# Weight tiles split two ahead, norm operands in two operations, and the first squares added on VectorE

## The chip, the cores and the metric

The kernel runs on one core of a Trainium2 chip. The metric is the device time of one launch in microseconds; it was 2138.77 us before (median of 3 runs, 2133.90 to 2140.38). The engines are named as in the profile: PE is TensorE (matrix multiplication), DVE is VectorE, ACT is ScalarE, POOL is GpSimd, SP issues the transfers between HBM and on-chip memory (SBUF). Each engine works through its own list of instructions in order and waits at an instruction until its inputs are there.

## What is computed

One inference step of a two-layer decoder, with width 1024, on a prompt of 512 rows and on 8 samples of 4 rows that have 256 earlier rows each in a paged cache. All of it is fp32. Cut to its structure:

```python
def trunk(x, pe, past):
    h = x
    for i in range(2):
        h = h + 0.5 * swiglu(rmsnorm(h, ffn1_norm[i]), w1, w3, w2)      # 1024 -> 2816 -> 1024
        xn = rmsnorm(h, mix_norm[i])
        if i == 0: mix = gmlp_mix(xn, w_in, v_norm, w_s, b_s, w_out)    # (u * spatial(v)) @ w_out
        else:      mix = forgetting_attention(rmsnorm(xn @ w_q), *kv, past) @ w_o
        h = h + mix
        h = h + 0.5 * swiglu(rmsnorm(h, ffn2_norm[i]), w1, w3, w2)
        h = h + sigmoid(rmsnorm(h, ple_norm[i]) @ w_gate) * (pe[i] @ w_proj)
        if i == 0: kv = shared_kv(h, kv_norm, w_kvf, b_f, k_norm)       # K, V, log-forget, once
    return h, kv

def rmsnorm(x, g): return x * rsqrt(mean(x * x) + 1e-6) * g
```

The outputs are h for the prompt and for the samples, K, V and the log-forget values of both, and the v rows of the gMLP for the samples.

## The kernel before, in words

Activations are kept feature-major: `h` is 8 chunks of 128 features by 544 columns (512 prompt rows and 32 sample rows, so both go through the weights together). A weight tile is 128 x 1024, eight blocks of 128 x 128, one for each chunk of the input.

An fp32 product is made of three passes with operands in two parts. The high part is the value rounded to the matrix engine's fp32r format, the low part is the remainder, and `mm` adds high x high (L233), high weight x low input (L237) and low weight x high input (L239), each in two column pieces (256 and 288): 48 matmuls for one tile of output. So each weight tile is *split* in the kernel, by a cast on ACT (L190) and a subtraction on DVE (L191), and so is each input (`split_pair`, L277 on ACT and L278 on DVE).

Weight tiles come in one stream for the whole program (`prepare`, `take`). `self.ahead` holds three distances, in tiles, counted from the tile that PE is about to use: how far ahead tiles are split, how far ahead the sums of tiles are made, and how far ahead raw tiles are loaded. Raw tiles, split tiles, inputs and chunks of `h` share one pool of 44 buffers of 128 x 1088 ("big" in the profile); a split 128 x 1024 tile takes two. A load on SP waits until its buffer is free, and everything behind it on SP waits with it.

The stages are: FFN 1 of layer A (0 to about 360 us), gMLP (to 590; its output tiles at 515 to 565), FFN 2, the gated embedding and the shared K/V (985 to 1126; tiles of V at 1061 to 1124), FFN 1 of layer B (to 1450), queries and attention (1490 to 1625), its output projection (1625 to 1702), FFN 2 and the embedding. The insides of the FFNs (Strassen-like, seven products for eight, with sums of weight tiles on DVE at L176) run in an order written by hand, with distances (2, 3, 6) of their own. Outside them a scheduler with a model of the engines sets the order.

A norm is applied in two halves. The gain goes into the input ahead of the product: `prep` makes the operand of a chunk as soon as the chunk of `h` is ready: it scales on ACT (L290) into a temporary, and splits that (L277, L278). The factor 1/sqrt(mean) goes onto the product afterwards. It comes from squares on ACT (L316), added up chunk by chunk on POOL (L318, `ssq`), the sum over partitions by PE (L354), and a chain ACT L332, DVE L335, L338, L339. At the start all 8 chunks of `h` are there at once, and the program does 8 preps and 8 squares together.

```python
box = {"x": {c: self.prep(h[c], G_FFN1 + c) for c in range(NC_)}, "f": [], "acc": self.st()}
self._split()
for c in range(NC_):
    self.ssq(box["acc"], h[c], first=c == 0)
```

Other lines that are spoken of: L418 and L484 (first steps behind the products of an FFN), L646 (gMLP output added to `h`), L750 and L769 (V and K taken out of PE's accumulators), L808 to L812 and L862 to L880 (log-forget sums), L941 (queries normed), L1144 to L1146 (the projection's three passes), L1156 and L1165 (its result added to `h`).

Of the kernel before, what the change touches and what calls it, by code (L numbers as in the profile page):

```python
# [22 lines left out]
F32 = mybir.dt.float32  # L23
F32R = mybir.dt.float32r
I32 = mybir.dt.int32
AF = mybir.ActivationFunctionType
ALU = mybir.AluOpType
# [54 lines left out]
def whole(p):  # L82

    return p[:].rearrange("p a b -> p (a b)")[:, 512 - CUT:512 - CUT + T]


class Builder:
# [37 lines left out]
    def set_stream(self):  # L125
        self.chain, self.pending, self.bg, self.pages = None, [], [], {}
        self.aps, self.raws = [], {}
        self.pieces, self.sums, self.split = [], {}, {}
        self.p_next = self.p_split = self.p_sum = self.a_load = 0
        self.ahead = (1, 1, 3)  # L130
        self.pins = 0

    def flat(self, n, dt=F32):
# [151 lines left out]
    def prep(self, h, gcol, pair=None, cols=slice(0, T)):  # L285

        pair = self.big(F32R) if pair is None else pair
        g = self.gain(gcol)
        x = self.tmp()[:, cols]
        self.nc.scalar.activation(x, h[:, cols], AF.Copy, scale=g)  # L290
        self.split_pair(pair, x, cols)
        return pair

    def forms(self, h, gcol, n, xs):
# [103 lines left out]
    def ffn(self, h, box, gcol, rstd, on_chunk):  # L398

        nc, eng = self.nc, mybir.EngineType  # L400
        self.ahead = (2, 3, 6)
        first, xs, xf = [], self.pairs(box), box["f"]

        def more(n):
            if len(xf) < min(n, NKP):
                xf.append(self.forms(h, gcol, len(xf), xs))
        for f in range(2):
            if rstd is None:
                p1, rstd = self.tile_rstd(xs, box["acc"])
            else:  # L410
                p1 = self.tile_mm(xs)
            more(2 * f + 1)
            p3 = self.tile_mm(xs)
            more(2 * f + 2)

            def gate(p1=p1, p3=p3):
                a, b = self.tmp(), self.tmp()
                nc.vector.tensor_tensor(a, whole(p1), rstd, ALU.mult)  # L418
                nc.scalar.activation(a, a, AF.Silu)
                nc.vector.tensor_tensor(b, whole(p3), rstd, ALU.mult)  # L420
                nc.vector.tensor_tensor(b, b, a, ALU.mult)
                pair = self.big(F32R)
                self.split_pair(pair, b)
                first.append((pair[:, 0, :], pair[:, 1, :]))
            self.evac(gate)
        assert len(first) == 2
        with self.tc.manual_schedule(engines={eng.PE, eng.Activation, eng.DVE, eng.Pool}):
            self.ffn_steps(h, xf, rstd, first, on_chunk)
        self.ahead = (1, 1, 3)
        self.pins = 2  # L430
        return rstd

# [741 lines left out]
    def build(self):  # L1174
        nc, i, o = self.nc, self.i, self.o
        self.set_stream()

        def plain(aps):
            for ap in aps:
                self.add_plain(ap)  # L1180

        def ple_units(n):
            for c in range(NC_):
                self.add_plain(i["wg"][n, c])
                if c < 2:
                    self.add_plain(i["wp"][n, c])

        self.ffn_pieces(0)
        plain([i["win"][NC_ + c] for c in range(NC_)] + [i["win"][c] for c in range(NC_)])
        plain(i["wout"][c] for c in range(NC_))  # L1190
        self.ffn_pieces(1)
        ple_units(0)
        plain([i["wf"]] + [i["wkv"][c] for c in range(2 * NC_)])
        self.ffn_pieces(2)
        plain(i["wq"][c] for c in range(NC_))
        plain([i["woh"][k, c] for k in range(2) for c in range(NC_ // 2)] + [i["wo"][c] for c in range(NC_)])
        self.ffn_pieces(3)
        ple_units(1)

        self.eps = self.const.tile([P, 1], F32, name="eps")  # L1200
        nc.vector.memset(self.eps, EPS)
        warm = self.sm(1)
        nc.scalar.copy(warm, self.eps)
        self._load()
        self.g = self.const.tile([P, NG], F32, name="gains")
        nc.scalar.dma_start(out=self.g, in_=i["gains"])
        hp = [self.big() for _ in range(NC_ // 2)]
        h = [hp[c // 2][:, c % 2, :] for c in range(NC_)]
        for c in range(NC_):
            nc.sync.dma_start(out=h[c], in_=i["x"][c])  # L1210
            if c == 2:
                self._load()
        self._split()
        self.ones = self.const.tile([P, 32], F32, name="ones")
        nc.gpsimd.memset(self.ones, 1.0)
        self.onesr = self.const.tile([P, P], F32R, name="onesr")
        nc.gpsimd.tensor_copy(self.onesr, self.ones[:, 0:1].broadcast_to([P, P]))
        self.c = self.const.tile([P, NCONST], F32, name="consts")
        self.pt = self.const.tile([1, NB * NPAGE], I32, name="pt")
        self.ident = self.c[:, C_ID:C_ID + P]  # L1220
        self.identr = self.const.tile([P, P], F32R, name="identr")
        self.neg = self.const.tile([P, 384], F32R, name="neg")
        self.ks = self.const.tile([P, NH, NS], F32, name="ks")

        box = {"x": {c: self.prep(h[c], G_FFN1 + c) for c in range(NC_)}, "f": [], "acc": self.st()}
        self._split()
        for c in range(NC_):
            self.ssq(box["acc"], h[c], first=c == 0)

        def constants():  # L1230
            yield
            nc.sync.dma_start(out=self.c, in_=i["consts"])
            nc.sync.dma_start(out=self.pt, in_=i["pt"])
            passed = self.big()[:].rearrange("p a b -> p (a b)")
            nc.sync.dma_start(out=passed[:, :NPASS], in_=i["passed"])
            yield
            nc.gpsimd.tensor_copy(self.identr, self.ident)
            nc.gpsimd.tensor_copy(self.neg, passed[:, C_NEG:C_NEG + 384])
        self.bg.append(constants())

        on, nxt = self.next_norm(h, G_MIX)
        self.ffn(h, box, G_FFN1, None, on)
        box = nxt
        on, nxt = self.next_norm(h, G_FFN2, early=3)
        self.gmlp(h, box, on)
        box = nxt
        on, nxt = self.next_norm(h, G_PLE)
        self.ffn(h, box, G_FFN2, None, on)
        box = nxt
        on, nxt = self.next_norm(h, G_KV)  # L1250
        self.bg.append(self.past())
        self.ple(h, box, 0, on)
        box = nxt
        box, rstd = self.kv(h, box, G_FFN1 + 8)
        on, nxt = self.next_norm(h, G_MIX + 8)
        self.ffn(h, box, G_FFN1 + 8, rstd, on)
        box = nxt
        on, nxt = self.next_norm(h, G_FFN2 + 8)
        self.attention(self.pairs(box), box["acc"], h, on)
        box = nxt  # L1260
        on, nxt = self.next_norm(h, G_PLE + 8)
        self.ffn(h, box, G_FFN2 + 8, None, on)
        box = nxt
        self.ple(h, box, 1, lambda c: nc.sync.dma_start(out=o["y"][c], in_=h[c]))
# [114 lines left out]
```

## Time and profile before

| | before |
|---|---|
| median of 3 runs | 2138.77 us (2133.90 to 2140.38) |
| profiled execution | 2137.89 us, span 2135.8 us, mean granted PE clock 0.988 |
| PE busy | 2078.1 us (97%), 57.7 us idle |
| DVE, ACT, POOL busy | 1523.3, 979.5, 179.2 us |
| chain that ended last | PE 89%, DVE 6%, ACT 3% |
| moved | 237.94 MB, mean 111 GB/s |

A row of waits reads: the instruction that waited, the releasing engine and tile and line; total us, times, the longest. A row of groups reads: line, engine, operation, shapes, how often, then busy us and the mean ns of one, then the idle time ahead of them and who ended it. A row of the timeline or the chain starts with the time and the length.

### The profile page before, as it was taken

To read this page: it belongs to the slowest core of one execution; us is meant where nothing else is said; L and a number is where in the kernel's file an instruction comes from. 1 tells how busy PE (TensorE), PEld (TensorE's weight loads), DVE (VectorE), ACT (ScalarE), POOL (GpSimd) and SP (SyncE) were. 2 spreads that over 40 slices of the span, in tenths; PEclk is the share of its full clock that TensorE was granted. 3 is DMA by queue.
4 is the path that set the end of the run, shared out by engine and by line. 5 is a ranking of instruction groups with operands and counts; after the bars stand their busy time and mean duration, and the time that the engine had idled before them with its cause. 6 is when DMAs were issued, how large, how long until landed. Compare 5 with 4: busy or idle time off the path is not lost.

```text
span 2135.8 us, 38870 instructions
## 1 busy us (share of the span) xinstructions
PE 2078.1 (97%) x16364; PEld 2033.1 (95%) x16364; DVE 1523.3 (71%) x1886; ACT 979.5 (46%) x1456; POOL 179.2 (8%) x233
## 2 busy tenths in 40 slices
PE   6999999999999999999989999999999899999999
PEld 5999999999999999999989999999876899999999
DVE  6877787556687777766688777786365687777864
ACT  6443344523544344465355344445264654443461
POOL 2000000310100000041140000001041300000010
PEclk9999999999999999999999999999999999999999
DMA  4232324312223222422183322326367322323331
GB/s 158 82 117 70 109 91 138 100 43 80 70 99 109 80 103 90 140 90 79 58 313 135 109 99 90 109 87 210 116 190 259 103 77 93 105 83 109 109 110 43
DMA packets 93776, 237.94 MB, mean 111 GB/s; under 512 B 9490, under 2 KB 27442, under 8 KB 93602
## 3 DMA queue, kind: packets, MB, share of 16 engines
q1 hardware_dynamic: 93458, 235.42, 33.2%
q8 instruction: 129, 2.11, 0.4%
q14 instruction: 45, 0.37, 0.1%
q10 hardware_dynamic: 144, 0.04, 0.0%
HBM read 218.94 MB, written 16.49 MB: 110 GB/s over the span
## 4 chain that ended last, share of the span: by engine, by line
PE 89%; DVE 6%; ACT 3%; issue 1%; DMA 1%; POOL 0%; SPq 0%; ACTq 0%; DVEq 0%; POOLq 0%
PE ps L476 33%; PE ps L233 14%; PE ps L239 14%; PE ps L237 14%; PE pb L476 5%; DVE big L278 1%; DVE big L191 1%; ACT big L190 1%; PE ps L1144 1%; PE ps L1146 1%; PE ps L1145 1%; DVE big L176 1%; ACT big L277 1%; PE ps L990 1%; PE ps L992 0%
## 5 line engine op out<-in xcount | busy, mean ns | idle before, releaser
L476 PE MATMUL ps<-big,big 128*128 128x272 f32 x5760 | 749.9, 289 | 10.1 <-ACT tmp L484 5.1
L476 PEld LDWEIGHTS ps<-big,big 128*128 128x128 f32 x5760 | 735.6, 189 | 11.7 <-ACT tmp L484 6.4
L191 DVE TENSOR_TENSOR big<-big,big 128x1024 fp32r<-128x1024 f32 (+2 forms) x541 | 596.7, 1106 | 102.0 <-ACT big L190 101.4
L190 ACT CAST big<-big 128x1024 fp32r<-128x1024 f32 (+2 forms) x541 | 489.4, 932 | 282.4 <-DVE big L176 275.9
L233 PE MATMUL ps<-big,big 128*128 128x256 f32 (+1 forms) x2768 | 580.6, 291 | 22.3 <-ACT big L277 11.5
L239 PE MATMUL ps<-big,big 128*128 128x256 f32 x2768 | 575.2, 290 | 6.4 <-DVE big L191 6.3
L237 PE MATMUL ps<-big,big 128*128 128x256 f32 x2768 | 577.4, 289 | 3.2 <-DVE big L278 3.1
L233 PEld LDWEIGHTS ps<-big,big 128*128 128x128 f32 x2768 | 447.6, 190 | 26.3 <-ACT big L277 12.0
L237 PEld LDWEIGHTS ps<-big,big 128*128 128x128 f32 x2768 | 451.1, 191 | 4.9 <-DVE big L278 4.9
L239 PEld LDWEIGHTS ps<-big,big 128*128 128x128 f32 x2768 | 446.9, 190 | 8.9 <-DVE big L191 8.2
L318 POOL TENSOR_TENSOR st<-st,tmp 128x544 f32<-128x544 f32 (+1 forms) x70 | 92.0, 1314 | 1644.8 <-ACT tmp L316 1644.2
L176 DVE TENSOR_TENSOR big<-big,big 128x1024 f32<-128x1024 f32 x160 | 195.1, 1219 | 0.0
L515 DVE SCALAR_TENSOR_TENSOR big<-ps,big 128x544 f32<-128x544 f32 x160 | 115.6, 723 | 95.5 <-PE ps L239 95.4
L278 DVE TENSOR_TENSOR big<-tmp,big 128x544 fp32r<-128x544 f32 (+1 forms) x132 | 108.7, 829 | 60.2 <-ACT big L277 59.0
L484 ACT COPY tmp<-ps 128x544 f32<-128x544 f32 x120 | 73.7, 614 | 146.0 <-PE ps L476 145.8
L476 PE MATMUL pb<-big,big 128*128 128x272 f32 x960 | 127.1, 288 | 0.0
L448 ACT ACTIVATE big<-big 128x544 f32<-128x544 f32 x80 | 52.8, 660 | 161.8 <-DVE big L445 160.4
L476 PEld LDWEIGHTS pb<-big,big 128*128 128x128 f32 x960 | 123.2, 188 | 0.0
L445 DVE TENSOR_TENSOR big<-big,st 128x1088 f32<-128x1088 f32 x80 | 103.3, 1291 | 9.9 <-ACT big L498 8.4
L290 ACT ACTIVATE tmp<-big,gains 128x544 f32<-128x544 f32 (+1 forms) x80 | 56.0, 703 | 115.7 <-DVE big L515 44.4
L277 ACT CAST big<-tmp 128x544 fp32r<-128x544 f32 (+1 forms) x132 | 80.6, 614 | 54.7 <-DVE tmp L303 21.5
L278 DVE TENSOR_TENSOR big<-big,big 128x544 fp32r<-128x544 f32 (+1 forms) x96 | 70.2, 731 | 29.0 <-ACT big L277 28.7
(185 smaller groups left out, 1257.8 us busy)
## 6 DMA issues: line engine op xcount, KB each, us to landing
big<-in_w SPq DMA_DIRECT2D x160, 512.0 KB
big<-in_w2a SPq DMA_DIRECT2D x64, 512.0 KB
big<-in_w2b SPq DMA_DIRECT2D x32, 384.0 KB
big<-in_w13p SPq DMA_DIRECT2D x16, 512.0 KB
big<-in_win SPq DMA_DIRECT2D x16, 512.0 KB
big<-in_wg SPq DMA_DIRECT2D x16, 512.0 KB
big<-in_wkv SPq DMA_DIRECT2D x16, 512.0 KB
big<-in_ck SPq DMA_DIRECT2D x16, 512.0 KB
```

The lines of the kernel that those rows point to most:

```text
L176: self.nc.vector.tensor_tensor(t, a, b, ALU.add if op == "+" else ALU.subtract)
L190: self.nc.scalar.copy(hi, src)
L191: self.nc.vector.tensor_tensor(lo, src, hi.bitcast(F32), ALU.subtract)
L233: i = nc.tensor.matmul(out[:, a:b], wh, xh[:, a:b], start=s, stop=False)
L237: nc.tensor.matmul(out[:, a:b], wh, xl[:, a:b], start=False, stop=False)
L239: nc.tensor.matmul(out[:, a:b], wl, xh[:, a:b], start=False, stop=e)
L277: self.nc.scalar.copy(pair[:, 0, cols], src)
L278: self.nc.vector.tensor_tensor(pair[:, 1, cols], src, pair[:, 0, cols].bitcast(F32), ALU.subtract)
L318: nc.gpsimd.tensor_tensor(acc[:, cols], acc[:, cols], sq, ALU.add)
L445: tt(g, g, rstd.unsqueeze(1).broadcast_to([P, 2, T]), ALU.mult)
L476: nc.tensor.matmul(dst[w], a[:, c], b, start=k in "152" and kp == 0 and n == 0, stop=kp == NKP - 1 and n == 2, skip_group_check=True)
L515: nc.vector.scalar_tensor_tensor(h[c], whole(out), 0.5, h[c], ALU.mult, ALU.add)
```

## The change

Three edits. Outside the FFNs the distances become (2, 2, 4) for (1, 1, 3): a tile is split two tiles before it is used, and loaded four before. `prep` takes two operations for three: ACT writes the scaled chunk straight into the fp32r high part (L289), and DVE makes the low part as `h * gain - high` in one operation (L290, with the gain as a column); the temporary is gone. And the 7 additions of the first squares go from POOL (L318) to DVE (L1231); their squares are now on L1229.

```diff
@@ set_stream, and the same again at the end of ffn @@
-        self.ahead = (1, 1, 3)
+        self.ahead = (2, 2, 4)
@@ prep @@
         pair = self.big(F32R) if pair is None else pair
         g = self.gain(gcol)
-        x = self.tmp()[:, cols]
-        self.nc.scalar.activation(x, h[:, cols], AF.Copy, scale=g)
-        self.split_pair(pair, x, cols)
+        self.nc.scalar.activation(pair[:, 0, cols], h[:, cols], AF.Copy, scale=g)
+        self.nc.vector.scalar_tensor_tensor(
+            pair[:, 1, cols], h[:, cols], g, pair[:, 0, cols].bitcast(F32), ALU.mult, ALU.subtract)
         return pair
@@ at the start @@
         for c in range(NC_):
-            self.ssq(box["acc"], h[c], first=c == 0)
+            sq = box["acc"] if c == 0 else self.tmp()
+            nc.scalar.activation(sq, h[c], AF.Square)
+            if c:
+                nc.vector.tensor_tensor(box["acc"], box["acc"], sq, ALU.add)
```

ACT has 1329 rows in place of 1409, DVE 1881 for 1873, POOL 199 for 206, SP 663 as before. Three places show how the order moves. The numbers in the names of buffers differ between the two programs; what counts is which buffer is used where.

The first is ACT at the start of the program (big_86 to big_89 hold the chunks of `h`, two each). Before:

```order
4 L290 ACTIVATE tmp_114<-big_86,gains 128x544
5 L316 ACTIVATE st_153<-big_86 128x544
6 L190 CAST big_100<-big_82 128x1024
7 L290 ACTIVATE tmp_119<-big_86,gains 128x544
8 L290 ACTIVATE tmp_124<-big_87,gains 128x544
9 L277 CAST big_113<-tmp_114 128x544
10 L277 CAST big_118<-tmp_119 128x544
...
24 L316 ACTIVATE tmp_168<-big_88 128x544
25 L277 CAST big_148<-tmp_149 128x544
...
29 L316 ACTIVATE tmp_177<-big_89 128x544
30 L190 CAST big_182<-big_180 128x1024
```

And after the change:

```order
4 L1229 ACTIVATE st_137<-big_86 128x544
5 L190 CAST big_100<-big_82 128x1024
6 L1229 ACTIVATE tmp_143<-big_86 128x544
7 L1229 ACTIVATE tmp_146<-big_87 128x544
8 L289 ACTIVATE big_113<-big_86,gains 128x544
9 L289 ACTIVATE big_116<-big_86,gains 128x544
...
19 L289 ACTIVATE big_134<-big_89,gains 128x544
20 L190 CAST big_138<-big_93 128x1024
21 L1229 ACTIVATE tmp_161<-big_89 128x544
22 L190 CAST big_166<-big_164 128x1024
```

The last square moves from row 29 to row 21, the last high part from row 25 to row 19, and three squares now stand ahead of the first operand where one did.

The second is DVE at the tiles of V: evacuations (L750, L769), the log-forget sums (L808 to L812, L862, L864), the norm's chain (L335 to L339) and splits of weights (L191). PE's row 6175 (low weight x high input, the fourth tile of V) reads big_11646 before. Before:

```order
876 L191 TENSOR_TENSOR big_11539<-big_11410,big_11538 128x1024
...
881 L812 SCALAR_TENSOR_TENSOR big_11010<-big_11326,big_11010 128x544
882 L335 SCALAR_TENSOR_TENSOR tmp_11616<-st_11615 128x544
883 L750 TENSOR_TENSOR tmp_11628<-ps_11556,st_11000 128x544
884 L769 SCALAR_TENSOR_TENSOR big_11074<-big_11074,gains,tmp_11467 128x544
...
888 L278 TENSOR_TENSOR big_11634<-big_11074,big_11634 128x512
889 L339 SCALAR_TENSOR_TENSOR st_11615<-tmp_11616,st_11615 128x544
890 L864 SCALAR_TENSOR_TENSOR sm_12213<-sm_12125,consts,sm_12213 128x8
891 L278 TENSOR_TENSOR big_11640<-tmp_11641,big_11640 128x544
892 L191 TENSOR_TENSOR big_11646<-big_11473,big_11645 128x1024
```

After the change PE's row 6175 reads big_11465:

```order
884 L191 TENSOR_TENSOR big_11465<-big_11336,big_11464 128x1024
...
889 L812 SCALAR_TENSOR_TENSOR big_10936<-big_11252,big_10936 128x544
890 L335 SCALAR_TENSOR_TENSOR tmp_11542<-st_11541 128x544
891 L750 TENSOR_TENSOR tmp_11554<-ps_11482,st_10926 128x544
892 L769 SCALAR_TENSOR_TENSOR big_11000<-big_11000,gains,tmp_11393 128x544
...
897 L339 SCALAR_TENSOR_TENSOR st_11541<-tmp_11542,st_11541 128x544
...
899 L290 SCALAR_TENSOR_TENSOR big_11566<-big_86,gains,big_11566 128x544
...
901 L191 TENSOR_TENSOR big_11570<-big_11399,big_11569 128x1024
```

The places of the splits among the other work are much the same, but each holds the next tile's: what PE's row 6175 needs is made ahead of the sums and the norm's chain (row 884) and no longer behind them (row 892).

The third is ACT in the output projection, where its first tiles over the sample columns and the rest of the half projections meet. Before, the second of those tiles (PE's row 9536) reads big_18711:

```order
1107 L290 ACTIVATE tmp_18682<-big_89,gains 128x272
1108 L316 ACTIVATE tmp_18686<-big_89 128x272
1109 L277 CAST big_18681<-tmp_18682 128x272
1110 L290 ACTIVATE tmp_18703<-big_89,gains 128x272
1111 L316 ACTIVATE tmp_18707<-big_89 128x272
1112 L290 ACTIVATE tmp_18742<-big_86,gains 128x272
1113 L316 ACTIVATE st_18466<-big_86 128x272
1114 L277 CAST big_18702<-tmp_18703 128x272
1115 L190 CAST big_18711<-big_18617 128x1024
```

After the change that tile (PE's row 9512) reads big_18544:

```order
1038 L190 CAST big_18499<-big_18344 128x1024
1039 L289 ACTIVATE big_18518<-big_88,gains 128x272
1040 L289 ACTIVATE big_18537<-big_88,gains 128x272
1041 L190 CAST big_18544<-big_18426 128x1024
1042 L316 ACTIVATE tmp_18444<-big_87 128x272
...
1046 L289 ACTIVATE big_18563<-big_89,gains 128x272
...
1048 L289 ACTIVATE big_18582<-big_89,gains 128x272
...
1050 L190 CAST big_18589<-big_18503 128x1024
```

The cast now stands ahead of the operands from big_89 (rows 1046 and 1048) and behind only those from big_88; before it stood behind those from big_89 and one from the next round of big_86 (row 1112), which wait for results of the projection itself.

More of the change, by code (lines that the diff above doesn't have):

```diff
@@ L428, in ffn @@
             self.ffn_steps(h, xf, rstd, first, on_chunk)
-        self.ahead = (1, 1, 3)
+        self.ahead = (2, 2, 4)
         self.pins = 2
```

## The prediction, on record before the result

> **What bounds the kernel now.** The page comes first (busy time and the chain that ended last), then what TensorE (PE) waited for, then the stretches in which it was not busy, at last single rows of those stretches.
>
> ```profile
> span 2135.8 us, 38870 instructions
> PE 2078.1 (97%) x16364; PEld 2033.1 (95%) x16364; DVE 1523.3 (71%) x1886; ACT 979.5 (46%) x1456; POOL 179.2 (8%) x233
> PE 89%; DVE 6%; ACT 3%; issue 1%; DMA 1%; POOL 0%; SPq 0%; ACTq 0%; DVEq 0%; POOLq 0%
> PE ps L233 <- ACT big L277: 11.5, 3, 9.7
> PE ps L233 <- ACT big L190: 9.4, 6, 3.0
> PE ps L239 <- DVE big L191: 6.3, 6, 2.9
> PE ps L1144 <- ACT big L190: 5.8, 4, 3.3
> PE ps L476 <- ACT tmp L484: 5.1, 6, 2.0
> PE ps L476 <- DVE tmp L418: 5.0, 1, 5.0
> PE ps L237 <- DVE big L278: 3.1, 4, 1.3
> PE ps L1146 <- DVE big L191: 1.5, 2, 1.2
> PE ps L781 <- DVE tmp L750: 0.9, 1, 0.9
> 0.00:53.00 53.00, 33.89 (x220) 31.42 (x220) 36.08 (x44) 36.19 (x54) 13.70 (x15) 0.91 0.46 159
> 107.00:500.00 393.00, 393.00 (x3144) 391.86 (x3142) 271.40 (x326) 162.28 (x231) 24.98 (x30) 1.00 0.29 95
> 515.00:565.00 50.00, 43.65 (x327) 42.33 (x326) 30.99 (x36) 26.93 (x40) 8.19 (x6) 0.97 0.26 85
> 985.00:1012.00 27.00, 25.47 (x190) 25.04 (x190) 18.54 (x22) 15.43 (x22) 5.50 (x4) 0.94 0.32 104
> 1061.00:1124.00 63.00, 55.74 (x404) 54.06 (x403) 52.84 (x74) 34.54 (x59) 26.44 (x28) 0.92 0.84 298
> 1500.00:1553.00 53.00, 49.45 (x344) 43.50 (x344) 21.39 (x28) 14.89 (x22) 0.31 (x1) 0.94 0.34 121
> 1625.00:1702.00 77.00, 68.69 (x465) 53.45 (x464) 43.30 (x75) 37.26 (x74) 20.67 (x48) 0.93 0.46 159
> ```
>
> PE is the bound: in 107:500 it is busy for all 393.00 us, 0.125 us a matmul at clock 1.00, and no split or operand is waited for. What is left to gain is 2135.8 − 2078.1 = 57.7 us of idle PE, and most of it lies in six stretches outside the FFN interiors (windows: length, busy us of PE, PEld, DVE, ACT, POOL, then granted clock, DMA share, GB/s). Two causes belong to this change: splits of weights (L190 the cast, L191 the remainder: 9.4 + 6.3 + 5.8 + 1.5 = 23.0) and operands of the norm (L277, L278: 11.5 + 3.1). A stall has a second price, the clock after it:
>
> ```profile
> 545.43:548.84 3.41, 3.41 (x17) 3.41 (x17) 2.05 (x2) 0.32 (x1) 0.33 (x1) 0.50 0.12 17
> 1002.82:1006.23 3.41, 3.41 (x18) 3.41 (x17) 1.75 (x2) 1.19 (x1) 0.00 (x0) 0.50 0.53 151
> 1071.09:1074.50 3.41, 3.41 (x18) 3.41 (x17) 3.39 (x9) 2.35 (x5) 1.45 (x2) 0.50 0.54 200
> 1094.98:1098.39 3.41, 3.41 (x16) 3.41 (x17) 3.41 (x5) 1.49 (x3) 2.73 (x2) 0.50 0.96 354
> 1112.05:1115.46 3.41, 3.41 (x17) 3.41 (x16) 3.09 (x5) 1.15 (x5) 0.00 (x0) 0.50 0.95 358
> 1531.89:1538.72 6.83, 5.34 (x21) 4.87 (x22) 3.05 (x3) 3.33 (x4) 0.00 (x0) 0.50 0.96 345
> 1665.01:1668.42 3.41, 3.35 (x16) 3.03 (x15) 2.19 (x3) 1.15 (x3) 3.33 (x6) 0.50 0.20 29
> 1675.25:1682.08 6.83, 6.36 (x26) 6.04 (x27) 4.99 (x5) 4.08 (x5) 0.00 (x0) 0.50 0.26 78
> ```
>
> In these the clock is 0.50: 17 matmuls take 3.41 us, 0.20 each against 0.125, and more so in their first. I price such a window at half of PE's busy time in it: 1.7 us, 2.7 for 1531.89, 3.2 for 1675.25.
>
> **The change, part by part.** The sum is made against the profiled execution, 2137.89 us (span 2135.8, 2.1 us around it), 0.9 under the median of 2138.77.
>
> ```profile
> L290 ACT ACTIVATE tmp<-big,gains 128x544 f32<-128x544 f32 x64 | 47.7, 749 | 83.5 <-DVE big L515 44.4 <-DVE big L646 23.6 <-DVE big L681 11.4
> L277 ACT CAST big<-tmp 128x544 fp32r<-128x544 f32 x116 | 74.3, 643 | 54.7 <-DVE tmp L303 21.5 <-DVE tmp L625 18.1 <-DVE tmp L421 8.3
> L278 DVE TENSOR_TENSOR big<-tmp,big 128x544 fp32r<-128x544 f32 x116 | 99.6, 862 | 55.1 <-ACT big L277 53.9
> L190 ACT CAST big<-big 128x1024 fp32r<-128x1024 f32 x381 | 393.6, 1047 | 282.4 <-DVE big L176 275.9 <-DMA big<-in_w13p 2.0 <-issue 1.6
> L316 ACT ACTIVATE tmp<-big 128x544 f32<-128x544 f32 x56 | 36.1, 651 | 25.9 <-DVE big L581 21.5 <-issue 4.4
> L191 DVE TENSOR_TENSOR big<-big,big 128x1024 fp32r<-128x1024 f32 x381 | 473.6, 1247 | 73.5 <-ACT big L190 72.9 <-DMA big<-kd 0.3
> L941 DVE SCALAR_TENSOR_TENSOR big<-big,gains,tmp 128x544 f32<-128x544 f32 x8 | 6.1, 781 | 1.0 <-DMA tmp<-rows 1.0
> 5.62 0.75 ACT tmp L290
> 15.70 12.73 POOL L318 TENSOR_TENSOR st<-st,tmp 128x544 f32<-128x544 f32 x7 [2.94 <-ACT tmp L316]
> 17.28 5.35 DVE L278 TENSOR_TENSOR big<-tmp,big 128x544 fp32r<-128x544 f32 x3 [2.10 <-ACT big L277]
> 34.48 0.88 ACT st L332 x2
> 1531.76 0.62 ACT L277 CAST big<-big 128x512 fp32r<-128x512 f32 x1 [2.56 <-DVE big L941]
> 1533.38 0.82 PE L233 MATMUL ps<-big,big 128*128 128x256 f32 x2 [3.02 <-ACT big L190]
> ```
>
> *Operands.* Each of the 64 whole preps loses one cast on ACT (643 ns) and keeps one pass of about 749. The DVE operation becomes one with a gain column; the nearest row for that form is L941's, 781 ns, while L278 runs at 862 on average, lengthened where POOL works. I take 0 for DVE; if every one of 64 grew by 0.06 us it would be 4 us of an engine that is 71% busy, hidden by PE outside the stretches below.
>
> *Start, −7.0 us (bounds −4 and −9).* Input arrives as before. ACT's work until the last square is 8 squares (0.65), 8 scaled operands (0.75) and two casts (1.05), 13.3 us from 5.6 (the first operand's start in the chain), so about 19. The seven POOL additions took 12.73 us until 28.43, and lengthened DVE's three remainders to 1.78 each (5.35). On DVE an addition takes at most the 0.78 of L941's form, and the last follows the last square, about 19.7. That is 8.7 us earlier, and the matmuls of the statistic stand earlier in PE's order. What PE must do before them gives back some: by laying the rows one behind the other L332 starts at 27.4 for 34.48, and DVE's chain from L335 to the last L418, which PE then waits for (5.0), is the same instructions. So 7; 4 if the matmuls ahead of the statistic take longer than laid out, 9 if the whole advance arrives. The first matmul, 9.7 us in, gains at most 1 of it.
>
> *gMLP output tiles, −8.0 (−4 to −8).* 515:565 has 50.00 − 43.65 = 6.35 us idle, all on L190/L191. The split of the tile after next now stands ahead of the same evacuation, a tile (48 matmuls, 6.0 us) of cover against single waits of under 2; plus one half-clock window, 1.7.
>
> *End of the first embedding stage, −2.5 (0 to −3.2).* 985:1012 idles 1.53 on L277/L278 and pays 1.7. Without the scaled copy the last operand is ready about 0.6 (a cast, 643 ns) earlier for the high part, and the low part follows it; a first wait of 0.5 goes, and half of the rest with its window as likely as not.
>
> *V tiles, −7.5 (−3 to −11.4).* 1061:1124 idles 7.26, of which 0.9 (L781) is another wait; 6.4 and three windows (5.1) make 11.4. The same matmul (row 6175 in both orders) has its remainder split on DVE at row 892 before, and now at row 884, before the logarithm's work. But DVE is busy 52.84 of 63 us, and 63 − 11.4 = 51.6 is below that: DVE can't be got under it, so at most 10 unless its own contention falls, and I take 7.5.
>
> *Query tiles, −5.5 (−3 to −5.7).* At 1533.38 PE waits 3.02 for a cast that stands behind L277, which waits for L941. The cast behind that operand (ACT row 972) is used by PE's row 8745; now the cast in that place (row 917) is used by PE's row 8793, a tile later (48 matmuls, 6.0 us). 3.0 + 2.7.
>
> *Output projection, −8.5 (−2 to −12.2).* 1625:1702 idles 8.31, 7.3 of it on L190/L191 (5.8 + 1.5), with windows of 1.7 and 3.2: 12.2. The longest (3.3) is a cast behind operands that wait for the previous projection; the split for that tile now stands before them. I leave off 3.7, since PE's order also changes here: more of the half projections come before the samples' last part, 55 matmuls between its two outputs instead of 36, and 204 after them instead of 228, so that DVE's and POOL's steps for the samples (POOL busy 20.67 in the stretch) have less behind them.
>
> *New waits, +4 (0 to +10).* Two split tiles hold one more pair, two of the 44 buffers, so loads that wait for a free one start later; DVE and ACT do a tile's split (1.25 and 1.05) ahead of other work in their queues. I take two new stalls of 1 us with a half window of 1 each. The order of loads on SP stays the same but for weights one place earlier; FFN interiors are the same by hand-written order, and the waits on L484 (5.1) and the start of FFN interiors remain.
>
> Sum: −7.0 − 8.0 − 2.5 − 7.5 − 5.5 − 8.5 + 4 = −35.0: **2137.9 − 35.0 = 2102.9, I say 2103.** The Trainium skill, "TensorE: Matmul & The Clock Gate", section on HAM oscillation, has as its rule that PE should have no idle gap over about 3.4 us, by which waits shorter than that would leave the clock alone. The trace disagrees: the window at 1071.09 follows one wait of 2.9 us. By the rule the terms would hold idle time alone, 7.0 + 6.4 + 1.2 + 4.2 + 3.0 + 5.1 − 2 = 24.9 of them, and the sum would be 2113.
>
> **Rivals.** *The whole ideal sum.* All these waits and all eight windows go: 9 + 8.0 + 3.2 + 11.4 + 5.7 + 12.2 = 49.5, 2088. For it: the waits name nothing else. Against it: DVE's 52.84 us at the V tiles. *DVE and the operands become the bound.* Where a split was waited for, the next late thing (an operand, an evacuation, DVE's queue) is right behind; only half of the V, projection, start and query terms comes, with all of the new waits: 7.0 + 8.0 + 7.5 + 5.5 + 8.5 = 36.5, half is 18, 2.5 falls away, 4 stays, so 14 or 2124. For it: DVE 71%, V tiles 84%. Against it: gMLP, where DVE has 19 of 50 us free. *The order does not move the late work.* The splits stay behind the same operands in the in-order queues and nothing but the start's 3 is gained: 2135. Against it: the rows of the order shown with the change. *Slower.* The buffers: with two fewer free, the reads of stored keys and values in the attention come late. DMA share is 0.96 in 1531.89:1538.72 already, so a late 512 KB read at 345 GB/s arrives 1.5 us late, and if each of 8 heads lost two such reads and a 6.83 us window (3.0 + 3.2), it cost 50 us: 2153 with the gains. It decides from the point where a head loses more than about 4 us (35 / 8). Against it: PE's waits name no such read now, and DMA share over the stage is 0.34.
>
> **The numbers.** Forecast (2103, its own range 2094 to 2112) 0.50; ideal 0.15; DVE bound 0.23; order without effect 0.07; slower 0.05. A measurement of this kernel tells about 0.3% (6.4 us) from no change: faster is under 2132.4. Forecast, ideal and DVE bound are all there, with a little of the fourth: 0.89; same 0.07; slower 0.04. The range leaves out one in ten at either end: 2090 (most of the ideal case is under it) to 2127 (just past the DVE case).
>
> **What would show it.** After: the rows of waits for L190 and L191 fall from 23.0 to under 5; 515:565 busy throughout; POOL without additions at the start, L332 near 27; clock 0.50 windows fewer by six or more; and the prep group as a DVE operation near 0.78. Wrong would be: the same idle time named for DVE's evacuations (L750, L1156) or for a read of kd; L332 still after 32; or as many windows at 0.50 as before.

## The result, and the profile after

The changed kernel takes **2090.97 us** (median of 4 runs, 2090.37 to 2091.88); the kernel before 2138.93 (4 runs). The ratio is 0.978, with a 95% interval of 0.976 to 0.980: 48 us or 2.2% faster. The forecast was 2103 with a range of 2090 to 2127, so the time lies in the range, 1 us above its lower end, and outside the forecast's own range (2094 to 2112). It is nearer to the rival in which every one of the waits goes (2088). The profiled execution took 2090.37 us; the comparisons of traces below are between it and the one before (2137.89).

The page of the kernel after, its span and the busy times:

```profile
span 2088.2 us, 38796 instructions
PE 2053.9 (98%) x16364; PEld 2016.3 (97%) x16364; DVE 1521.5 (73%) x1893; ACT 934.8 (45%) x1376; POOL 181.0 (9%) x226
```

The span is 47.6 us shorter, and only half of it is idle PE: 57.7 us before, 2088.2 − 2053.9 = 34.3 now, so 23.4 less. The other 24.2 is *busy* PE that went away with the number of matmuls unchanged (16364). What PE waits for after the change, by releaser (total, times, longest):

```profile
PE ps L233 <- ACT big L289: 8.8, 1, 8.8
PE ps L476 <- DVE tmp L418: 5.3, 1, 5.3
PE ps L476 <- ACT tmp L484: 5.2, 6, 2.0
PE ps L233 <- ACT vs L786: 1.9, 3, 0.8
PE ps L1145 <- POOL big L1133: 1.8, 1, 1.8
PE ps L1144 <- DVE big L1156: 1.5, 2, 0.9
PE ps L239 <- DVE big L191: 1.0, 1, 1.0
PE ps L781 <- ACT big L277: 0.8, 1, 0.8
PE ps L233 <- DVE tmp L669: 0.7, 1, 0.7
```

Of 23.0 us on L190 and L191 one wait of 1.0 is left. New are the small ones on L786, L1133 and L669. The first operand (8.8) and the two FFN waits (5.3, 5.2) stand as they did. The stretches of before, in the kernel after (length, busy us of PE, PEld, DVE, ACT, POOL, clock, DMA share, GB/s):

```profile
0.00:45.65 45.65, 30.39 (x220) 29.23 (x220) 35.17 (x51) 31.73 (x46) 3.17 (x8) 0.97 0.47 166
508.46:558.46 50.00, 50.00 (x404) 50.00 (x403) 35.60 (x41) 27.02 (x38) 11.57 (x7) 1.00 0.22 75
1041.00:1095.00 54.00, 51.30 (x416) 49.44 (x411) 50.17 (x72) 28.74 (x50) 29.71 (x31) 1.00 0.88 313
1478.00:1515.00 37.00, 36.89 (x280) 32.87 (x279) 16.59 (x21) 10.30 (x15) 0.31 (x1) 1.00 0.48 172
1588.00:1655.00 67.00, 63.66 (x484) 51.23 (x483) 45.43 (x77) 32.35 (x61) 21.75 (x50) 1.00 0.54 185
```

The gMLP stretch is busy throughout, with 404 matmuls in 50 us instead of 327. At the V tiles DVE is busy 50.17 of 54 us. The mean granted clock went from 0.988 to 0.997: 15 stretches of 3.41 us at half clock before (the long ones of 6.83 counted as two), 3 after.

Where the time went, by stage. The gain at a landmark is the start of one and the same instruction before, less its start after; the gain of a stage is the difference between its landmark and the last one. The last column is what the prediction would have had if every wait that it names, and the half clock behind it, had gone.

| stage, up to the landmark | before | after | gain | forecast | all waits and clock |
|---|---|---|---|---|---|
| start and FFN 1, first L598 | 461.89 | 454.53 | 7.4 | 7.0 | 9 |
| gMLP, L354 of the norm behind it | 574.85 | 558.41 | 9.1 | 8.0 | 8.0 |
| FFN 2 and first embedding tiles, fifth L681 | 984.79 | 969.50 | −1.1 | part of −4 | 0 |
| end of the embedding and K, last L735 | 1053.63 | 1034.99 | 3.3 | 2.5 | 3.2 |
| V tiles, an L484 of the next FFN | 1302.68 | 1274.25 | 9.8 | 7.5 | 11.4 |
| queries and attention, first L1156 | 1596.24 | 1561.01 | 6.8 | 5.5 | 5.7 |
| projection, next L354 | 1705.41 | 1657.97 | 12.2 | 8.5 | 12.2 |
| to the end | 2121.44 | 2073.91 | 0.1 | 0 | 0 |

The sum is 47.5.

### The profile page after: what moved, and what is told of

It is laid out like the page before. It is cut to its first block, busy times and chain, and to the rows that moved or that the text cites. A ratio compares the mean times of both kernels' runs of the same rounds, so it can differ in the third digit from the quotient of the medians.

```text
span 2088.2 us, 38796 instructions
## 1 busy us (share of the span) xinstructions
PE 2053.9 (98%) x16364; PEld 2016.3 (97%) x16364; DVE 1521.5 (73%) x1893; ACT 934.8 (45%) x1376; POOL 181.0 (9%) x226
## 4 chain that ended last, share of the span: by engine, by line
PE 88%; DVE 5%; ACT 3%; DMA 2%; issue 1%; SPq 0%; POOL 0%; ACTq 0%; DVEq 0%; POOLq 0%
PE ps L476 33%; PE ps L233 14%; PE ps L239 14%; PE ps L237 14%; PE pb L476 5%; ACT big L190 1%; DVE big L191 1%; DVE big L176 1%; PE ps L1144 1%; PE ps L1146 1%; PE ps L1145 1%; PE ps L992 0%; PE ps L990 0%; PE ps L1105 0%; DMA big<-in_w13p 0%
## 5 line engine op out<-in xcount | busy, mean ns | idle before, releaser
L191 DVE TENSOR_TENSOR big<-big,big 128x1024 fp32r<-128x1024 f32 (+2 forms) x541 | 594.6, 1101 | 107.9 <-ACT big L190 107.7
L190 ACT CAST big<-big 128x1024 fp32r<-128x1024 f32 (+2 forms) x541 | 489.4, 932 | 282.5 <-DVE big L176 275.3
L233 PE MATMUL ps<-big,big 128*128 128x256 f32 x2768 | 576.2, 289 | 12.0 <-ACT big L289 8.8
L239 PE MATMUL ps<-big,big 128*128 128x256 f32 x2768 | 570.9, 288 | 1.0 <-DVE big L191 1.0
L237 PE MATMUL ps<-big,big 128*128 128x256 f32 x2768 | 571.2, 287 | 0.1
L233 PEld LDWEIGHTS ps<-big,big 128*128 128x128 f32 x2768 | 443.5, 189 | 15.4 <-ACT big L289 8.8
L239 PEld LDWEIGHTS ps<-big,big 128*128 128x128 f32 x2768 | 442.8, 188 | 1.8 <-DVE big L191 1.2
L318 POOL TENSOR_TENSOR st<-st,tmp 128x544 f32<-128x544 f32 (+1 forms) x63 | 87.3, 1386 | 1610.9 <-ACT tmp L316 1610.6
L484 ACT COPY tmp<-ps 128x544 f32<-128x544 f32 x120 | 73.5, 612 | 146.5 <-PE ps L476 146.2
L289 ACT ACTIVATE big<-big,gains 128x544 fp32r<-128x544 f32 (+1 forms) x80 | 55.9, 703 | 118.9 <-DVE big L515 64.9
L278 DVE TENSOR_TENSOR big<-big,big 128x544 fp32r<-128x544 f32 (+1 forms) x96 | 69.5, 724 | 29.0 <-ACT big L277 28.6
L290 DVE SCALAR_TENSOR_TENSOR big<-big,gains,big 128x544 fp32r<-128x544 f32 (+1 forms) x80 | 64.6, 810 | 21.8 <-ACT big L289 21.8
L277 ACT CAST big<-big 128x544 fp32r<-128x544 f32 (+1 forms) x96 | 61.9, 644 | 27.0 <-DVE big L769 15.2
```

The costliest lines, as they stand in the source:

```text
L190: self.nc.scalar.copy(hi, src)
L191: self.nc.vector.tensor_tensor(lo, src, hi.bitcast(F32), ALU.subtract)
L233: i = nc.tensor.matmul(out[:, a:b], wh, xh[:, a:b], start=s, stop=False)
L237: nc.tensor.matmul(out[:, a:b], wh, xl[:, a:b], start=False, stop=False)
L239: nc.tensor.matmul(out[:, a:b], wl, xh[:, a:b], start=False, stop=e)
L278: self.nc.vector.tensor_tensor(pair[:, 1, cols], src, pair[:, 0, cols].bitcast(F32), ALU.subtract)
```

## The experiments

The theory at this point, A: each stall goes with the edit that moves the work it names, so the edits add up. The rival, B: they overlap, since fewer operations on ACT also let the splits come sooner. Gains by stage below are taken at the same landmarks, in the profiled run of each kernel, against the kernel before.

**Each edit alone.** The kernel before with only `self.ahead = (2, 2, 4)`:

```diff
-        self.ahead = (1, 1, 3)
+        self.ahead = (2, 2, 4)
```

> The kernel before with only the distances (2, 2, 4) outside the FFNs. Theory A (each stall goes with the edit that moves the work it names; after against before the stages gained 9.1 at the gMLP output tiles, 3.4 at the end of the embedding, 9.8 at the V tiles, 6.8 at the queries, 12.2 at the projection, 7.4 at the start): the rows of L190 and L191 go, so gMLP, V tiles, queries and projection gain their 9.1 + 9.8 + 6.8 + 12.2 = 37.9, less about 1 of new waits; start and embedding stay as before. 2139 - 37 = 2102 us. Theory B (the edits overlap: the shorter operands let ACT and DVE reach the splits in time, and the lookahead alone leaves the splits behind the longer operands): at most 28 us gained, 2111 or more, with waits on L277 in place of L190.

2101.04 us, ratio 0.983 (0.981 to 0.985): 37 us. By stage: start 0.1, gMLP 9.3, FFN 2 −1.5, embedding 3.6, V 8.3, queries 3.8, projection 11.4. The time is theory A's; the embedding's 3.6 is not, since its waits were on operands. At the queries the 3.0 us less than the changed kernel's 6.8 are clock alone: between the two landmarks PE idles 1.0 us in either, and this profile has a half-clock stretch of 6.83 us there (from 1531.40) where the changed kernel has none.

The kernel before with only the new `prep`:

```diff
-        x = self.tmp()[:, cols]
-        self.nc.scalar.activation(x, h[:, cols], AF.Copy, scale=g)
-        self.split_pair(pair, x, cols)
+        self.nc.scalar.activation(pair[:, 0, cols], h[:, cols], AF.Copy, scale=g)
+        self.nc.vector.scalar_tensor_tensor(
+            pair[:, 1, cols], h[:, cols], g, pair[:, 0, cols].bitcast(F32), ALU.mult, ALU.subtract)
```

> The kernel before with only the operand in two operations. Theory A: the wait on L277/L278 at the end of the embedding goes (3.4), and at the start, where ACT loses 8 casts of 0.64 before the last square, about 2 of the 7.4; the waits on L190/L191 stay: 2139 - 5 = 2134 us. Theory B: the splits of weights come earlier too wherever they stand behind operands (gMLP, V tiles, queries, projection), so half of the 37.9 comes as well: 2120 us or less.

2122.04 us, ratio 0.992 (0.990 to 0.994): 16 us, between the theories. By stage: start 4.1, gMLP −1.1, embedding 0.7, V 1.2, queries −0.9, projection **11.3**. So B holds in one place, the projection, and nowhere else. PE's waits there:

```profile
PE ps L233 <- ACT big L190: 8.7, 7, 3.2
PE ps L239 <- DVE big L191: 6.4, 6, 1.9
PE ps L1144 <- ACT big L190: 1.7, 2, 1.3
PE ps L1146 <- DVE big L191: 0.8, 1, 0.8
```

L233 and L239 wait for splits as they did (9.4 and 6.3 before), L1144 only 1.7 for 5.8. The order says why: with one ACT operation for an operand the scheduler sets the cast for the second projection (ACT row 1049) ahead of the next round's operand from big_86 (row 1051), where before it stood behind it (rows 1115 and 1112). And the embedding needs the lookahead: before, the first K tile's 16 instructions of L233 all stand ahead of the second tile's; with the lookahead both tiles' weights are split, and the order takes matmuls of the second while the last operand of the first is late. The L233 by accumulator, in PE's order (before, then lookahead alone):

```
16 ps_10947   16 ps_11025
12 ps_10953   2 ps_11031   2 ps_10953   4 ps_11031   2 ps_10953   10 ps_11031
```

The kernel before with only the additions on DVE:

```diff
-            self.ssq(box["acc"], h[c], first=c == 0)
+            sq = box["acc"] if c == 0 else self.tmp()
+            nc.scalar.activation(sq, h[c], AF.Square)
+            if c:
+                nc.vector.tensor_tensor(box["acc"], box["acc"], sq, ALU.add)
```

> The kernel before with only the seven additions moved from POOL to DVE. Theory A: the start alone changes; the sum of squares is done some 6 us earlier than 28.43 and DVE's remainders fall from 1.78 to about 0.75, so 5 us of the 7.4 come: 2134 us, stall on L418 still there. Theory B: ACT's three operations a chunk keep the squares late, and the start gains under 2: 2137 us.

2132.42 us, ratio 0.998 (0.997 to 0.999): 5 us by the medians, and in the trace 3.5 at the start and 0.4 or less in any other stage. Theory A, with a smaller advance: DVE's remainders do fall from 1.78 to 0.73 us, but the sum is done at 24.1 us, 4.3 earlier and not 6, and L332 starts at 30.77 for 34.48.

**Each edit taken out of the changed kernel.**

Without the lookahead:

```diff
-        self.ahead = (2, 2, 4)
+        self.ahead = (1, 1, 3)
```

> The changed kernel with the distances back at (1, 1, 3). Theory A: loses the 37 us that the lookahead is worth, 2128 us, with L190/L191 waits of about 20 us. Theory B (overlap with the operands): loses 25 or less, 2116 us or less.

2115.28 us (2113.78 to 2120.05): loses 24, where the lookahead alone had brought 37. By stage it keeps 6.8 at the start and 11.3 at the projection, and little is left of gMLP (2.0 of 9.1), embedding (0.7), V (3.3) and queries (0.3), where PE waits for L190 and L191 again (18.1 us in the whole kernel). That is the overlap again: the projection comes with either edit. The three edits alone bring 37 + 16 + 5 = 58 us and together 48, and their profiled gains at the projection alone are 11.4 + 11.3 + 0.1 against 12.2. Theory A falls for this stage, and for the embedding, whose gain came with the lookahead and not with the operands that its waits named. It holds for gMLP, V and the queries, as far as the clock lets one see (below).

Without the operands in two operations:

```diff
-        self.nc.scalar.activation(pair[:, 0, cols], h[:, cols], AF.Copy, scale=g)
-        self.nc.vector.scalar_tensor_tensor(...)
+        x = self.tmp()[:, cols]
+        self.nc.scalar.activation(x, h[:, cols], AF.Copy, scale=g)
+        self.split_pair(pair, x, cols)
```

> The changed kernel with operands in three operations again. Theory A: loses the 3.4 at the end of the embedding and about 2 at the start: 2096 to 2097 us. Theory B: loses 10 or more, with splits late again in projection and queries: 2101 us or more.

2095.85 us (2095.50 to 2096.13): loses 4.9, as A had it, but at other places: start 3.7 and V 1.2, nothing at the embedding (3.6 is kept). So the time is A's by luck.

Without the additions on DVE:

```diff
-            if c:
-                nc.vector.tensor_tensor(box["acc"], box["acc"], sq, ALU.add)
+            self.ssq(box["acc"], h[c], first=c == 0)
```

> The changed kernel with the seven additions on POOL again. Theory A: only the start changes: the sum ends near 26, L332 comes about 5 us later, 2096 us. Rival: with the operands in two operations the squares are early enough and the additions on POOL cost under 2: 2092 us.

2095.07 us (2093.26 to 2099.11): loses 4.1, 3.9 of it at the start in the trace and 1.5 at the projection, where this run had one half-clock stretch more. With prep alone the start gains 4.1, with the additions alone 3.5, with all three edits 7.4 (6.8 without the lookahead): there the times nearly add up. The path is not the expected one. The sum ends at 21.9 and not near 26, and L332 comes at 28.32, 1.5 us after the changed kernel's 26.87 and not 5. Most of the loss comes behind it: from L335 to the first L418 DVE takes 5.85 us (29.22 to 35.07) where the changed kernel takes 3.09, because a weight split and two remainders of operands now stand among the norm's chain. Nor do the starts of L332 add up: 34.48 before, 27.65 with prep alone, 30.77 with the additions alone. Why the scheduler sets DVE's order so is not shown.

**The distances one by one,** and beyond.

```diff
-        self.ahead = (2, 2, 4)
+        self.ahead = (2, 2, 3)
```

> The changed kernel with distances (2, 2, 3): split two ahead, loaded three ahead as before, so a raw tile has one tile of time (6 us) from its load to its split instead of two. If the split distance alone is what matters: 2091 us, within 2. If the loads are as needed: splits wait for DMA (a 512 KB tile takes 3.5 us at the start, and more where DMA is 0.9 busy, at the V tiles), 5 us or more slower, most of it at the V tiles and the queries.

2099.81 us (2099.22 to 2100.25): 8.8 slower than the change. The V tiles keep 4.8 of 9.8 and the projection 10.7 of 12.2; FFN 2 of layer B loses 1.3, the start 1.3 and the queries 1.0. The splits' place in the order is not enough without the earlier load: at the V tiles a cast now waits for its weights (ACT, timeline), if only for 0.4 us, and PE's waits there on evacuations, which stand behind such work in the queues, are longer than the changed kernel's 1.9 and 0.8. The 5 us are these two waits (0.9 and 1.5 more), waits at the entry of the next FFN on L418 and L484 (2.4 us for 1.3), and one half-clock stretch (at 1128.61, 1.5 us by the price below): 5.0 in all. That the late load stands at the root of each of them is argued from the edit; no single wait names it.

```profile
1090.62 1.05 ACT L190 CAST big<-big 128x1024 fp32r<-128x1024 f32 x1 [0.40 <-DMA big<-in_w13p]
```

```profile
PE ps L233 <- ACT vs L786: 2.8, 3, 1.5
PE ps L781 <- DVE tmp L750: 2.3, 1, 2.3
```

```diff
-        self.ahead = (2, 2, 4)
+        self.ahead = (1, 1, 4)
```

> The changed kernel with distances (1, 1, 4): loads as in the changed kernel, splits one ahead as before. If the split distance is what matters: as without any lookahead, 2115 us, within 3. If earlier loads do a part: 2110 us or less.

2119.55 us (2116.23 to 2120.26), against 2115.28 with (1, 1, 3): earlier loads alone bring nothing. By stage its gains are those of the operands alone (gMLP −1.1, V 1.0, queries −1.1, projection 11.4). Of the three distances the split decides, and the load has to follow it.

```diff
-        self.ahead = (2, 2, 4)
+        self.ahead = (3, 3, 5)
```

> The changed kernel with the distances (3, 3, 5): three split tiles, one more pair of buffers. Theory A: hardly a wait on a split is left (1.0 us in the changed kernel), so nothing to gain: 2091 us, within 3. Rival (buffers): two buffers fewer for the reads of keys, values and weights; waits on reads or splits appear in the attention and the projection and it is slower by 3 to 15 us.

2094.92 us (2093.49 to 2095.85): 4 us slower than (2, 2, 4). It loses 5.9 against the kernel before in the stretch from FFN 2 to the first embedding tiles, where the changed kernel loses 1.1. DVE's timeline there, and what PE waited for:

```profile
936.07 1.50 DVE L191 TENSOR_TENSOR big<-big,big 128x1024 fp32r<-128x1024 f32 x1
937.49 1.78 DVE L339 SCALAR_TENSOR_TENSOR st<-tmp,st 128x544 f32<-128x544 f32 x1
939.38 1.99 DVE L669 TENSOR_TENSOR tmp<-ps,st 128x544 f32<-128x544 f32 x3
```

```profile
PE ps L233 <- DVE tmp L669: 2.9, 1, 2.9
```

A split stands inside the norm's chain, between L338 and L339, and PE's accumulators are freed only behind L339. In the changed kernel the same split stands there, at nearly the same lengths, for 0.7 us of waiting; before, none did:

```profile
932.96 1.50 DVE L191 TENSOR_TENSOR big<-big,big 128x1024 fp32r<-128x1024 f32 x1
934.38 1.81 DVE L339 SCALAR_TENSOR_TENSOR st<-tmp,st 128x544 f32<-128x544 f32 x1
```

So the split accounts for what the two kernels share. The other 2.2 us of the wait come from further ahead: the statistic's last matmuls (L354) stand later in PE's order, so that PE runs out of other work 8.5 us behind them (928.75 to 937.26) where the changed kernel has 10.0 (926.37 to 936.37), and DVE's chain from L354 to L669 is 0.7 longer. Most of the rest of the 4.7 us between the kernels is a half-clock stretch and some 1.3 us that only cross the landmark (gMLP gains 10.4 for 9.1). No wait of PE in this run names a read or a load, which speaks against the buffers.

**Buffers.** The changed kernel with four buffers fewer:

```diff
-NBIG = 44
+NBIG = 40
```

> The changed kernel with 40 buffers instead of 44. If the buffers that the second split pair takes have a price, twice as many taken away must show it: new waits for reads in the attention or for weights, 3 us or more (2094 us or more). If the pool has room, within 2 of 2091 us.

2092.29 us (2090.07 to 2092.44): the same within what the measurement tells. The pool has room, and the mechanism of the rival on the slower side doesn't act here, even with four buffers taken away where the change takes two.

**Two places mended.**

```diff
         for c in range(NC_):
             nc.sync.dma_start(out=h[c], in_=i["x"][c])
             if c == 2:
                 self._load()
+        self._load()
+        self._load()
@@ ple @@
         for c in range(NC_ + 2):
+            self.ahead = (1, 1, 3) if c < 3 else (2, 2, 4)
```

> The changed kernel with two places mended that its profile names. (1) At the start the third and fourth weight tiles are loaded before the cached pages' addresses are read on SP, not at 15.77 us behind them; if the start's chain is held by that load (its cast waits 2.41 us for it), the statistic's chain comes 1.5 to 2.5 us earlier, and if the sum of squares or PE's work holds it, under 0.5. (2) In the embedding the distances are (1, 1, 3) for the first three tiles, so that no split stands between L338 and L339 of the norm's chain; if that split is the cause of the new wait on L669 (0.7 us) the 1.1 us that the changed kernel loses there come back, and if not, nothing. Together 2091 - 3 = 2088 us, below the changed kernel.

2089.04 us (5 runs, 2088.53 to 2091.85), 0.978 of before (0.976 to 0.979): no measurable difference to the changed kernel. In the trace the wait on L669 is gone and the stretch up to the fifth L681 loses 0.2 instead of 1.1, which confirms the split inside the chain as the cause of this wait. The start gains 0.3 only. The load was late, as the timeline of the changed kernel shows (ACT and DVE),

```profile
19.33 1.05 ACT L190 CAST big<-big 128x1024 fp32r<-128x1024 f32 x1 [2.41 <-DMA big<-in_w13p]
20.29 0.64 ACT L349 CAST tmp<-st 128x544 fp32r<-128x544 f32 x1
23.96 0.65 ACT L277 CAST big<-tmp 128x544 fp32r<-128x544 f32 x1 [0.30 <-DVE tmp L306]
24.52 1.05 ACT L190 CAST big<-big 128x1024 fp32r<-128x1024 f32 x1
25.58 1.28 ACT L332 ACT_TABLE_LOAD   x1
26.87 0.87 ACT L332 ACTIVATE st<-pb,eps 128x272 f32<-128x272 f32 x2
```

```profile
18.73 0.71 DVE L1231 TENSOR_TENSOR st<-st,tmp 128x544 f32<-128x544 f32 x1
```

but L332 stands in ACT's queue behind operands (L277) and a cast, and these set its time: with the load early it comes at 26.2 instead of 26.9. What the two places give in the trace is taken back in the projection (10.7 for 12.2), where this profile has one half-clock stretch more at the same order of matmuls and the same idle time (4.0 us).

## Why the prediction was right, and where it was off

*The bound and the causes.* PE was the bound, and the waits named for L190 and L191 were the ones that went: 23.0 to 1.0 us, as the forecast's test had it (under 5). Twelve of 15 half-clock stretches went (six or more were forecast).

*Operands, DVE at 0.* Right. The new DVE operation takes 840 ns on average with a gain column (781 was the nearest row), where L278 took 862 in the group from temporaries:

```profile
L290 DVE SCALAR_TENSOR_TENSOR big<-big,gains,big 128x544 fp32r<-128x544 f32 x64 | 53.5, 840 | 19.1 <-ACT big L289 19.1
```

ACT is busy 979.5 − 934.8 = 44.7 us less, about the 64 casts.

*Start, −7.0.* 7.4 came, and the times named came too: the last addition ends at 19.4 (forecast 19.7), L332 is at 26.9 (27.4), and the stall on L418 remains at 5.3. But the step said that PE's work ahead of the statistic gives back some of the advance. The statistic's last matmuls (L354) start at 24.82 and 24.94; what holds L332 after them is ACT's own queue, as the rows above show. So the 27.4 was near by some luck. The step also didn't name that half of the gain belongs to the operands: 4.1 with them alone, 3.5 with the additions alone.

*gMLP, −8.0.* 9.1, above the upper bound. The bound was mis-sized: it priced a stall at its idle time and the half clock, and a third price was missing. Between the second and the eighth evacuation (L646) the kernel before takes 45.5 us and after 35.8. Of the 9.7 us, 6.35 are idle, 1.5 the one half-clock stretch, and 1.8 is left, 0.3 for each of 6 waits, in which PE was counted as busy. The records show where most of it sits: the matmul ahead of each of these waits is recorded as 0.29 or 0.30 us long, although in a dense stream the next one starts 0.125 us after it, and the first one behind the wait takes 0.22 until the next starts: 0.17 + 0.10 us a wait.

*Embedding, −2.5.* 3.3 came, but the step failed: it was said to come from the operands in two operations. With these alone it is 0.7, with the lookahead alone 3.6, by the second tile's matmuls that fill the wait. The operands alone do shorten the waits that the step named (PE's idle time in the stage falls from 1.53 to 0.49 us) and no half-clock stretch is left there, yet PE is counted as busy for 67.7 us of it, against 65.5 in the changed kernel; that this is all short waits is not shown.

*V tiles, −7.5.* 9.8 came, 2.3 more. The stretch now stands near the floor that DVE's work sets (it is busy 93% of the 54 us, and the three waits on L786 and the one on L781 are what is left, 2.7 us), but that floor left more room than taken. The loads, named as "one place earlier" and given no price, are worth 5 of the 9.8 (1.5 of them a half-clock stretch).

*Queries, −5.5.* 6.8; the wait behind L941 is gone, the stretch is busy for 36.89 of 37 us.

*Projection, −8.5.* 12.2, the whole ideal. The 3.7 left off for the changed order of PE was the largest single error. The new waits that it feared came (L1132 and L1133, 2.4 us together, behind POOL), but the old ones and three half-clock stretches were worth more. In part it is the luck of this profile: two kernels with the same order of matmuls there and the same 4.0 us of idle time, the one with the additions on POOL and the one with two places mended, have one half-clock stretch in the projection and gain 10.7. That the lookahead was needed here was wrong: either of two edits gives 11.

*New waits, +4.* They are inside the stages' gains, apart from FFN 2 and the embedding, where 1.1 is lost. The cause was named (a split ahead of other work in a queue), the place was not. Buffers had no price.

*The rivals.* The sum of the second rival, in which DVE and the operands become the bound, halves gMLP's 8.0 although its words leave that stage whole; with it whole the gain is 18 us and that rival stands at 2120, not at 2124. The time that came is nearest to the first rival, 2088. The V tiles, where the prediction held DVE's work against that one, came 1.6 us short of it (9.8 for 11.4).

So the bound and the signs held, and the mechanism at gMLP, the V tiles and the queries; the embedding's and in part the start's and the projection's were other than said. The 12 us between 2103 and 2091 are the terms' sizes: projection 3.7, new waits about 3, V 2.3, queries 1.3, gMLP 1.1, embedding 0.8 and start 0.4. Of the 24.2 us that came as busy time, 18 are half clock (12 stretches at 1.53 us, below). The rule of the Trainium skill weighed in the prediction ("TensorE: Matmul & The Clock Gate", HAM oscillation), read there so that waits under 3.4 us leave the clock alone, isn't borne out: in the kernel before, the stretches at 545.43, 1002.82, 1094.98, 1112.05 and 1665.01 follow waits of 1.5 us and less.

## What to carry to other kernels

A short wait of the bottleneck engine is worth more than its length: in this kernel 23.4 us of idle time took another 24.2 us with it, so price a stall at about twice its idle time before calling it small. Where several edits may cure the same stall, run each alone and each left out: the projection's 11 us came with either of two, and one stage's gain belonged to the edit that had not been credited with it. A split further ahead needs its load as far ahead, and it can land in a chain on which the bottleneck waits: that cost 0.7 us at two tiles ahead, and one step more lost 4 us.

## What the runs showed of the hardware that was not expected

The half clock follows waits, but not each time. The kernel with the operands alone and the one with operands and additions have the same PE order through the gMLP output tiles, and the same idle time there; the first has two half-clock stretches in it and the second none (windows over the same 50 us of each):

```profile
509.00:559.00 50.00, 44.55 (x325) 43.24 (x324) 31.44 (x37) 23.37 (x33) 10.40 (x6) 0.94 0.26 85
```

```profile
505.00:555.00 50.00, 44.54 (x347) 43.23 (x346) 32.64 (x38) 24.39 (x35) 10.20 (x6) 1.00 0.25 85
```

PE idles 5.45 and 5.46 us, at clock 0.94 and 1.00, and between the first and the last evacuation of the stage the first kernel needs 3.06 us more: 1.53 us for each stretch of 3.41 (the prediction had 1.7). Single profiles of kernels with such waits differ by a few of these; the difference of 4 us between distances (1, 1, 4) and (1, 1, 3) goes with 8 half-clock stretches against 5. The projection shows the same once more: 4.0 us of idle time each, 96.96 us without a stretch and 98.50 with one. What decides whether a wait draws one was not tried.

By these prices the busy time nearly closes: 12 stretches fewer at 1.53 are 18.4 us, and 5.8 of the 24.2 remain. PE has 20 waits over 0.15 us where it had 40, and 20 fewer at the 0.27 us that the records around a wait show make 5.4.
